# One gated hybrid decoder step on one core: shorter first steps of the triangular inverses, a guard folded into a multiplication, and two copies that change engines

## The chip, the core and the metric

The kernel runs on one core of a Trainium2 chip. The core has a matrix engine (TensorE, "PE" in the profile, with its weight loads listed apart as "PEld"), a vector engine (VectorE, "DVE"), a scalar engine for activation functions (ScalarE, "ACT"), a general engine (GpSimd, "POOL"), and a queue that issues transfers (SyncE, "SP"). They share an on-chip memory of 128 partitions (SBUF); matmuls write to a second one, PSUM, whose banks of 128 x 512 numbers are handed around by this program as buffers. The metric is the time of one execution on the device in microseconds, as a median over runs.

## The reference, cut to what matters

One layer is computed for a prompt of 1024 tokens and for eight samples of one token each. Width is 1024. A projection `p = x @ w_in` feeds a gated linear attention (GLA, 4 heads), an RWKV-7 recurrence (16 heads of 64) and two sigmoid gates; the two branches go through their own up-projections, are gated and added, pass an output product, and a layer norm ends it. The change lies in the RWKV branch:

```
w  = exp(-0.606531 * sigmoid(w0 + tanh(w_lr) @ w2));   a = sigmoid(a0 + a_lr @ a2)
kk = kb * k_k                                     # per head of 64 channels
kk = kk / maximum(sqrt(sum(kk**2)), 1e-12)
kb = kb * (1 + (a - 1) * k_a)
S_t = S_{t-1} (diag(w_t) - kk_t^T (kk_t * a_t)) + v_t^T k_t ;   y_t = S_t r_t
```

followed by a group norm of y, a bonus term and a gate.

## The kernel before, in words

**Tiling.** The tokens go in two passes: the first 512 prompt tokens with the eight samples (520 columns), then the other 512. Channels lie on the 128 partitions, tokens along the free dimension. A matmul with more precision than one multiplication of rounded numbers gives is made from two parts: the operand is rounded (the high part) and the rounding error is kept (the low part); the projections use three products, `hi*hi`, `hi*lo`, `lo*hi`. `split` (line 468) makes such a pair of parts: a copy that rounds, and a subtraction.

**The RWKV branch** works on pairs of heads: 8 pairs in each pass, 16 in all, each with 128 channels. `pair` (line 1111) runs four parts in turn.

- `front` (line 1135) makes the decay, the key norm and the operands of the chunked recurrence, in chunks of 64 tokens. `te` is the squared scaled key; `head_sums` (line 483) splits it and sums over each head by two matmuls with a matrix of ones, into a PSUM bank of the kind `big`, of which there are four. Line 1169 takes the larger of the sum and 1e-24, out of PSUM into `te`; then a logarithm and an exponential on ScalarE give the inverse square root (lines 1173 and 1174), scaled by 65536 under the logarithm. Line 1177 multiplies keys, `nkk` (the negated key scale `k_k`) and the inverse norm into `ta`; lines 1179 and 1180 make from it the first half of `AZ` and `td`.
- Still in `front`, Gram products of the chunks give triangular matrices, and their 32 x 32 diagonal blocks are gathered into a layout in which each partition holds one block. There, lines 1224 to 1229 invert all blocks at once in 31 steps: step j multiplies rows 0 to j of the inverse so far, cut into groups of which `ni = j // 4 + 1` are touched, by a row of the matrix (into `Xt`), and adds the product.
- `back` and `turn` join the blocks to 64 x 64 inverses and transpose operands.
- `chain` (line 1300) runs the recurrence over 8 chunks, each after the other: a matmul with the decayed products, its copy `rh` out of PSUM (line 1318), a matmul with the inverse, a copy to `u`, a matmul for the state, and the state update on VectorE. Copies of the state (`ss`, `s0p`) are ScalarE's.
- `norm` ends the pair and sends it to `o_rwkv` in device memory.

**Order.** Nothing is ordered by the hardware's choice alone. Each part above is a stream that yields instructions; `Order.run` (line 377) takes at each turn the stream whose next instruction can start first by its own estimated costs (`price`, line 145), corrected by a priority of the stream, and appends that instruction to its engine's list. So a changed instruction may change the order of all that is drawn after it, on every engine. `self.V`, `self.A` and `self.P` are VectorE, ScalarE and TensorE. `self.E` lets the planner choose VectorE or GpSimd for an instruction, and `self.C` ScalarE or VectorE, by which would end first by its estimate, where VectorE must be ahead of ScalarE by 0.1 us (`BIAS`). Activation functions belong to table sets; a change of set costs a table load on ScalarE (line 401), and sigmoid and exponential lie in different sets. Projection blocks are drawn between the steps of the chains and of the GLA heads, in PSUM banks of their own (`proj`).

Nearly all instructions are recorded at line 217, the helper that makes them, so groups of the profile are told apart by the names of their tiles.

Of the kernel before, what the change touches and what calls it, by code (L numbers as in the profile page):

```python
# [14 lines left out]
AF = mybir.ActivationFunctionType  # L15
ALU = mybir.AluOpType
# [16 lines left out]
C = 64  # L33
# [63 lines left out]
KK_SCALE = 65536.0  # L97
# [325 lines left out]
class Kern(Order):  # L423
# [41 lines left out]
        o, w = CST[name]  # L465
        return self.cons[:, o:o + w]

    def split(self, x, tag="part"):

        hi, lo = (t[:x.shape[0], :x.free_size()] for t in (yield from self.get(tag, 2)))  # L470
        yield self.C.copy(hi, x)
        yield (self.V if x.space == PSUM else self.E).tensor_sub(lo, x, hi.bitcast(F32))
        return hi, lo

# [5 lines left out]
    def blocks32(self, x):  # L480
        return x.rearrange("p (j f) -> p j f", f=32)

    def head_sums(self, x):

        hi, lo = yield from self.split(x)
        ps = yield from self.bank("big", [P, HT])
        yield from self.sums(ps, self.headsr, hi, lo)
        self.free(hi, lo)
        return ps
# [6 lines left out]
    def setup(self):  # L496
        nc, a = self.nc, self.a
        E = mybir.EngineType
        self.es.enter_context(self.tc.manual_schedule(engines={E.PE, E.Activation, E.DVE, E.Pool, E.SP}))
        cp = self.pool("const")  # L500
        wp = self.pool("w", side="left")
        self.dr = self.pool("dr", space=DRAM)
        pp = self.pool("psum", space=PSUM)
        xp = self.pool("x", side="right")
        self.r1 = r1 = self.pool("work", side="left")
        for tag, bufs in BANKS.items():
            self.buffers(tag, bufs, lambda tag=tag, bufs=bufs: pp.tile([P, 512], F32, name=tag, bufs=bufs))
        for tag, (shape, bufs) in SBUF.items():
            dt = F32R if tag in PARTS else F32
            self.buffers(tag, bufs, lambda tag=tag, shape=shape, bufs=bufs, dt=dt:  # L510
                         r1.tile(shape, dt, name=tag, bufs=bufs))
        for tag, (shape, bufs) in WBUF.items():
            dt = F32 if tag == "wraw" else F32R
            self.buffers(tag, bufs, lambda tag=tag, shape=shape, bufs=bufs, dt=dt:
                         wp.tile(shape, dt, name=tag, bufs=bufs))
        self.buffers("xs", XS, lambda: xp.tile([P, HALF], F32R, name="xs", bufs=XS))
        nc.scalar.preload_act_table_set(EXP)
        self.cons = cp.tile([P, CST_W], F32, name="cons")
        self.pv = cp.tile([P, PV_W], F32, name="pv")
        self.ident = self.cst("ident")  # L520
        self.omu = cp.tile([P, NRC], F32, name="omu")
        self.oka = cp.tile([P, 8], F32, name="oka")
        self.nkk = cp.tile([P, 8], F32, name="nkk")
        self.bias = {}
        for n, v in [("glaeps", GLA_EPS), ("gneps", GN_EPS), ("lneps", LN_EPS), ("one", 1.0),
                     ("kkl", 0.5 * math.log(KK_SCALE))]:
            t = cp.tile([P, 1], F32, name="b_" + n)
            nc.vector.memset(t, v)
            self.bias[n] = t
        dbg = getattr(self, "dbg", {})  # L530
        self.o_gla = dbg.get("o_gla", None) or self.dr.tile([D, T], F32, name="o_gla")
        self.o_rwkv = dbg.get("o_rwkv", None) or self.dr.tile([D, T], F32, name="o_rwkv")
        self.sg = [[[self.dr.tile([P, PASS[i][1]], F32, name=f"sg{i}{n}{k}") for k in range(NK)] for n in range(2)]
                   for i in range(2)]
        self.mg = [[self.dr.tile([P, PASS[i][1]], F32, name=f"mg{i}{k}") for k in range(NK)] for i in range(2)]

        self.lev = cp.tile([P, 2 * B32 * MASKED], U8, name="lev")

        self.onesr = cp.tile([P, P], F32R, name="onesr")
        self.headsr = cp.tile([P, P], F32R, name="headsr")  # L540
        self.wa = cp.tile([P, NK * 16], F32, name="wa")
        self.alr = cp.tile([96, HALF], F32R, name="alr")
        self.gw2 = cp.tile([96, GH * GDK], F32R, name="gw2")

        self.GS = [self.dr.tile([P, GDV], F32, name=f"GS{h}") for h in range(GH)]
        self.Sp = [self.dr.tile([P, C], F32, name=f"Sp{n}") for n in range(NPAIR)]

        self.smp = cp.tile([P, 4, NPAIR, NS], F32, name="smp")
        self.RS = self.dr.tile([4, NS, D], F32, name="RS")
        self.WA = self.dr.tile([2, NS, D], F32, name="WA")  # L550
        self.tail = cp.tile([P, NS + 1, NRC], F32, name="tail")
        self.carry = cp.tile([P, NRC], F32, name="carry")
        self.shT = cp.tile([P, NRC, NS], F32, name="shT")
        self.reset = cp.tile([P, HT], U8, name="reset")
        nc.vector.memset(self.reset, 1)
        nc.vector.memset(self.reset[:, ::C], 0)


        for tag, n, bufs in (("XT", 2 * HT, 2), ("X1", HT, 1), ("X2", HT, 1)):
            ts = [cp.tile([P, n], F32, name=f"{tag}{i}") for i in range(bufs)]  # L560
            for t in ts:
                nc.gpsimd.memset(t, 0.0)
            self.fixed(tag, ts)
# [571 lines left out]
    def front(self, c, p, st, d):  # L1135
        a, A, V, E = self.a, self.A, self.V, self.E
# [3 lines left out]
        AZ = az.rearrange("p (c k t) -> p c k t", c=NCH, k=2)  # L1140
# [11 lines left out]
        r, kb, v = (x[:, :HT] for x in st)  # L1152
        def bc(ap):
            return ap.rearrange("p (c t) -> p c t", t=C)
# [10 lines left out]
        yield from lora(pa, 1)  # L1165
        yield A.activation(td, pa, AF.Sigmoid, bias=self.pvec("a0", p))
        self.free(pa, l2h, l2l)
        ps = yield from self.head_sums(te)
        yield V.tensor_scalar(te, ps, 1e-24, None, ALU.max)
        self.free(ps)  # L1170
        yield V.tensor_tensor_scan(tb, self.reset, ta, 0.0, ALU.mult, ALU.add)
        yield E.memset(Pc[:, :, 0:1], 1.0)
        yield A.activation(te, te, AF.Ln, scale=KK_SCALE)
        yield A.activation(te, te, AF.Exp, scale=-0.5, bias=self.bias["kkl"])
        yield A.activation(Pc[:, :, 1:], bc(tb), AF.Exp, scale=-LAM)
        yield A.activation(tb, tb, AF.Exp, scale=LAM)
        yield V.scalar_tensor_tensor(ta, kb, self.nkk[:, p:p + 1], te, ALU.mult, ALU.mult)
        yield A.activation(te, td, AF.Identity, scale=self.pvec("ka", p), bias=self.oka[:, p:p + 1])
        yield E.tensor_mul(AZ[:, :, 0], bc(ta), Pc[:, :, 0:C])
        yield V.scalar_tensor_tensor(td, td, -1.0, ta, ALU.mult, ALU.mult)  # L1180
        yield E.tensor_mul(kb, kb, te)
        yield E.tensor_mul(AZ[:, :, 1], bc(r), Pc[:, :, 1:])
        pc = yield from self.get("pc")
# [39 lines left out]
        tm = yield from self.get("Xt")  # L1223
        for j in range(31):
            w, ni = 31 - j, j // 4 + 1
            tv = tm[:, :ni * w].rearrange("p (s t) -> p s t", t=w)
            yield V.tensor_mul(tv, X[:, 0:ni, j:j + 1].to_broadcast([P, ni, w]),
                               L[:, j:j + 1, j + 1:].to_broadcast([P, ni, w]))
            yield V.tensor_add(X[:, 0:ni, j + 1:], X[:, 0:ni, j + 1:], tv)
# [70 lines left out]
    def chain(self, c, p, d):  # L1300
# [12 lines left out]
        for x in range(NCH):  # L1313
            u = u_[:, x]
            pr = yield from self.bank("pch", [P, 2, C])
            yield self.P.matmul(pr, GG[:, x, 0], u, start=True, stop=True)
            rh = yield from self.get("rh")
            yield V.tensor_copy(rh, pr)
            self.free(pr)
            s0p = None  # L1320
            if x >= first:
                for h, hs in enumerate(HS):
                    yield A.copy(ss[hs, x], u[hs, h])
                s0p = yield from self.get("s0p")
                yield A.activation(s0p, ss[:, x], AF.Copy, scale=pc[:, x:x + 1])
            pu = yield from self.bank("pch", [P, 2, C])
            yield self.P.matmul(pu, XT[:, x], rh, start=True, stop=True)
            self.free(rh)
            for h, hs in enumerate(HS):
                yield self.C.copy(u[hs, h], pu[hs, h])  # L1330
            self.free(pu)
            pS = yield from self.bank("pch", [P, 2, C])
            yield self.P.matmul(pS, bt_[:, x], u, start=True, stop=True)
            for h, hs in enumerate(HS):
                un = u_[hs, x + 1, h] if x + 1 < NCH else S[hs]
                if s0p is None:
                    yield V.tensor_scalar(un, pS[hs, h], pc[hs, x:x + 1], None, ALU.mult)
                else:
                    yield V.scalar_tensor_tensor(un, pS[hs, h], pc[hs, x:x + 1], s0p[hs], ALU.mult, ALU.add)
            self.free(pS, *([] if s0p is None else [s0p]))  # L1340
# [499 lines left out]
```

## Time and profile before

| | |
|---|---|
| median of 3 runs | 1490.67 us (1490.38 to 1747.76) |
| the profiled execution | 1487.92 us |
| its span, first to last instruction | 1486.1 us |
| mean granted TensorE clock | 0.996 |
| instructions | 31563 |
| transfers | 318.96 MB in 211258 packets, mean 215 GB/s |

The span is the time between the first and the last instruction of the profiled execution; the execution's own time has some microseconds around it. In the views below, a row of a group gives: line, engine, operation, the tile written and the tiles read (buffer numbers left out), shapes, the count, the busy time in microseconds with the mean of one in nanoseconds, and the idle time of the engine just before, with what ended most of it. A row of the windows gives the busy time of each engine within a stretch of the span. A busy PE is not PE at its peak: matmuls are pipelined and their ends are modelled. Idle time of an engine that is not the bottleneck costs nothing.

The chain of waits that ended last names PE for most of its length from 1034 us on; the longest pieces of it after 1290 us are runs of 24 to 72 matmuls of the output products.

### The profile page before, as it was taken

The page shows a single profiled execution, that of the slowest core. Times are in us where ns is not written, and L with a number is a line of the kernel's source. Part 1 is how long each engine was busy: PE and PEld are TensorE (multiplying, and loading weights), DVE is VectorE, ACT ScalarE, POOL GpSimd, SP SyncE. Part 2 cuts the span into 40 slices and gives each one's busy share as a digit, 9 for nine tenths or more (in the row PEclk, how much of TensorE's full clock was granted, in tenths as well). Part 3 has the DMA queues.
Part 4 walks back from the last instruction along what each step waited for, and adds up shares of the span by engine and source line. Part 5 has one row for each costly group of instructions (what it writes and reads, how often), then busy time and mean ns, then how long its engine had stood idle before and what let it go on. Part 6 is the DMA issues. An engine that isn't in the chain of part 4 may idle for free. (4 is left out here: it accounts for less than half of the span.)

```text
span 1486.1 us, 31563 instructions
## 1 busy us (share of the span) xinstructions
PE 1449.8 (98%) x11158; PEld 1260.4 (85%) x11158; DVE 1194.8 (80%) x3255; ACT 857.7 (58%) x2196; POOL 113.6 (8%) x208
## 2 busy tenths in 40 slices
PE   9999999999999999999999999999999999999997
PEld 6998999899989998787777777878787898988786
DVE  6697889888998899879878989898877866755665
ACT  5666776676767776665754555474547645544210
POOL 1001010201010102000101020111001000000000
PEclk9999999999999999999999999999999999999999
DMA  8886786678676877566566556656564766888432
GB/s 299 273 285 202 250 296 214 226 253 295 202 258 211 294 229 258 170 224 188 160 198 179 155 190 191 192 154 188 174 189 138 229 210 221 295 293 271 139 107 85
DMA packets 211258, 318.96 MB, mean 215 GB/s; under 512 B 91811, under 2 KB 107180, under 8 KB 211100
## 3 DMA queue, kind: packets, MB, share of 16 engines
q1 hardware_dynamic: 211100, 316.93, 66.8%
q8 instruction: 89, 1.46, 0.4%
q14 instruction: 69, 0.57, 0.1%
HBM read 197.19 MB, written 118.61 MB: 212 GB/s over the span
## 5 line engine op out<-in xcount | busy, mean ns | idle before, releaser
L217 PE MATMUL proj<-xs,wpart 128*128 128x264 f32 (+2 forms) x5640 | 1017.7, 327 | 1.4 <-DVE row L217 0.8
L217 PEld LDWEIGHTS proj<-xs,wpart 128*128 128x128 f32 x5640 | 808.5, 189 | 80.3 <-issue 9.9
L217 ACT CAST wpart<-wraw 128x512 fp32r<-128x512 f32 x210 | 130.2, 623 | 103.5 <-PE proj L217 49.6
L217 DVE TENSOR_TENSOR row<-row 128x512 f32<-128x512 f32 (+7 forms) x321 | 166.3, 524 | 12.4 <-ACT row L217 5.6
L217 DVE TENSOR_TENSOR wpart<-wraw,wpart 128x512 fp32r<-128x512 f32 x207 | 145.2, 702 | 32.3 <-ACT wpart L217 31.4
L217 ACT ACTIVATE row<-row 128x512 f32<-128x512 f32 (+5 forms) x213 | 128.8, 610 | 14.4 <-DMA row<-sg 6.5
L217 POOL TENSOR_TENSOR row<-row 128x512 f32<-128x512 f32 (+5 forms) x64 | 72.7, 1143 | 746.3 <-DVE row L217 396.4
L217 DVE TENSOR_TENSOR Xt<-X,wide 128x60 f32<-128x60 f32 (+24 forms) x496 | 104.8, 211 | 11.7 <-DMA wide<-LD 1.8
L217 DVE TENSOR_TENSOR X<-X,Xt 128x60 f32<-128x60 f32 (+24 forms) x496 | 105.4, 213 | 10.0
L217 ACT ACTIVATE row<-proj,omu 128x256 f32<-128x256 f32 (+1 forms) x99 | 54.0, 546 | 93.5 <-PE proj L217 93.3
L217 PE MATMUL big<-xs,wpart 128*128 128x256 f32 (+2 forms) x576 | 101.7, 332 | 0.0
L217 PEld LDWEIGHTS big<-xs,wpart 128*128 128x128 f32 x576 | 87.7, 194 | 9.7 <-issue 0.2
L217 DVE SCALAR_TENSOR_TENSOR wide<-pch,pc,s0p 64x64 f32<-64x64 f32 x208 | 58.7, 282 | 32.9 <-PE pch L217 28.0
L217 ACT COPY row<-wide 64x64 f32<-64x64 f32 x240 | 57.9, 241 | 40.2 <-DVE wide L217 34.7
L401 ACT ACT_TABLE_LOAD x62 | 79.5, 1283 | 1.1
L217 DVE SCALAR_TENSOR_TENSOR row<-proj,pv,row 128x255 f32<-128x255 f32 (+1 forms) x99 | 56.3, 569 | 22.4 <-ACT tail L217 13.7
L217 PE MATMUL big<-row 128*32 128x32 f32 (+4 forms) x936 | 65.3, 241 | 1.4 <-ACT row L217 1.4
L217 ACT COPY row<-big 128x128 f32<-128x128 f32 (+6 forms) x134 | 38.7, 318 | 42.2 <-PE big L217 36.7
L217 ACT COPY wide<-pch 64x64 f32<-64x64 f32 x159 | 32.8, 206 | 47.0 <-PE pch L217 45.1
L217 ACT ACTIVATE row<-proj 128x128 f32<-128x128 f32 (+4 forms) x136 | 36.9, 324 | 37.4 <-PE proj L217 37.0
L217 PE MATMUL pch<-wide,gg 128*128 128x128 f32 x256 | 51.6, 283 | 5.5 <-DVE wide L217 4.7
L217 PEld LDWEIGHTS pch<-wide,gg 128*128 128x128 f32 x256 | 42.3, 189 | 16.1 <-PE proj L217 4.7
(249 smaller groups left out, 1992.6 us busy)
## 6 DMA issues: line engine op xcount, KB each, us to landing
w<-wpart SPq DMA_DIRECT2D x146, 512.0 KB
wpart<-w SPq DMA_DIRECT2D x146, 512.0 KB
wraw<-w_in SPq DMA_DIRECT2D x146, 256.0 KB
wide<-LD SPq DMA_DIRECT2D x64, 128.0 KB
wraw<-w_up_gla SPq DMA_DIRECT2D x32, 256.0 KB
wraw<-w_up_rwkv SPq DMA_DIRECT2D x32, 256.0 KB
sg<-row SPq DMA_DIRECT2D x16, 260.0 KB
row<-sg SPq DMA_DIRECT2D x16, 260.0 KB
```

Of the source, the lines that this page charges most:

```text
L217: ways.append((eng, lambda call=call: call(out, *args, **kw), price(eng, name, out, args, ins)))
L401: self.nc.scalar.preload_act_table_set(self.table)
```

## The change

Four edits, all in the RWKV branch.

1. **Inverse.** In steps 0 to 3, where one group of rows is touched, the multiplication into `Xt` and the addition become one `scalar_tensor_tensor` on VectorE: row j of the matrix times the j-th entry of the inverse's first row in that partition (a per-partition multiplier), plus the running row.
2. **Guard.** The maximum with 1e-24 goes. The logarithm reads the sums straight from PSUM, with a bias of 65536 x 1e-34; the bank is freed behind it. The guard is now a minimum with 1e12 on the inverse norm, inside the multiplication that makes `ta`; `ta` no longer holds `-k_k`, and that factor moves into the multiplications for the first half of `AZ` (a `scalar_tensor_tensor` on VectorE instead of a multiplication on VectorE or GpSimd) and for `td`.
3. **High part.** In the first `head_sums` of a pair the high part is no longer a rounding copy of `te` but a second Square of the keys on ScalarE, written in the rounded type.
4. **rh.** Its copy may go to ScalarE or VectorE, as the planner finds, instead of VectorE always.

```diff
-    def split(self, x, tag="part"):
+    def split(self, x, tag="part", high=None):
         hi, lo = (t[:x.shape[0], :x.free_size()] for t in (yield from self.get(tag, 2)))
-        yield self.C.copy(hi, x)
+        yield high(hi) if high else self.C.copy(hi, x)
         yield (self.V if x.space == PSUM else self.E).tensor_sub(lo, x, hi.bitcast(F32))
...
-    def head_sums(self, x):
-        hi, lo = yield from self.split(x)
+    def head_sums(self, x, high=None):
+        hi, lo = yield from self.split(x, high=high)
...
-                     ("kkl", 0.5 * math.log(KK_SCALE))]:
+                     ("kkl", 0.5 * math.log(KK_SCALE)), ("kkt", KK_SCALE * 1e-34)]:
...
-        ps = yield from self.head_sums(te)
-        yield V.tensor_scalar(te, ps, 1e-24, None, ALU.max)
-        self.free(ps)
+        ps = yield from self.head_sums(te, lambda hi: A.activation(hi, kb, AF.Square, scale=self.pvec("kk", p)))
         yield V.tensor_tensor_scan(tb, self.reset, ta, 0.0, ALU.mult, ALU.add)
         yield E.memset(Pc[:, :, 0:1], 1.0)
-        yield A.activation(te, te, AF.Ln, scale=KK_SCALE)
+        yield A.activation(te, ps, AF.Ln, scale=KK_SCALE, bias=self.bias["kkt"])
+        self.free(ps)
         yield A.activation(te, te, AF.Exp, scale=-0.5, bias=self.bias["kkl"])
...
-        yield V.scalar_tensor_tensor(ta, kb, self.nkk[:, p:p + 1], te, ALU.mult, ALU.mult)
+        yield V.scalar_tensor_tensor(ta, te, 1e12, kb, ALU.min, ALU.mult)
         yield A.activation(te, td, AF.Identity, scale=self.pvec("ka", p), bias=self.oka[:, p:p + 1])
-        yield E.tensor_mul(AZ[:, :, 0], bc(ta), Pc[:, :, 0:C])
-        yield V.scalar_tensor_tensor(td, td, -1.0, ta, ALU.mult, ALU.mult)
+        yield V.scalar_tensor_tensor(AZ[:, :, 0], bc(ta), self.nkk[:, p:p + 1], Pc[:, :, 0:C], ALU.mult, ALU.mult)
+        yield V.scalar_tensor_tensor(td, td, self.pvec("kk", p), ta, ALU.mult, ALU.mult)
...
         for j in range(31):
             w, ni = 31 - j, j // 4 + 1
+            if ni == 1:
+                yield V.scalar_tensor_tensor(X[:, 0, j + 1:], L[:, j, j + 1:], X[:, 0, j:j + 1], X[:, 0, j + 1:], ALU.mult, ALU.add)
+                continue
...
-            yield V.tensor_copy(rh, pr)
+            yield self.C.copy(rh, pr)
```

## The prediction

> **What bounds the kernel now.** I read the page first: the busy shares of the engines over the whole span.
>
> ```profile
> span 1486.1 us, 31563 instructions
> PE 1449.8 (98%) x11158; PEld 1260.4 (85%) x11158; DVE 1194.8 (80%) x3255; ACT 857.7 (58%) x2196; POOL 113.6 (8%) x208
> ```
>
> The matmuls leave 36.3 us of the span without PE work (1486.1 - 1449.8). A share over the whole span hides the stages, so the second view is the windows view, cut where the stages change: the body with projections, chains and GLA heads; the hundred microseconds of the last chain; the output products; the tail.
>
> ```profile
> 100.00:1200.00 1100.00, 1078.19 (x8751) 938.67 (x8750) 944.10 (x2750) 693.70 (x1827) 105.65 (x187) 1.00 0.67 210
> 1200.00:1300.00 100.00, 96.04 (x805) 92.24 (x804) 67.77 (x151) 55.19 (x110) 0.00 (x0) 0.97 0.77 248
> 1300.00:1440.00 140.00, 140.00 (x606) 111.09 (x605) 84.55 (x130) 48.05 (x100) 0.37 (x1) 1.00 0.63 210
> 1440.00:1486.00 46.00, 38.45 (x189) 31.93 (x188) 24.37 (x41) 1.99 (x8) 2.77 (x3) 0.96 0.26 86
> ```
>
> Columns: length, then busy time of PE, PEld, DVE, ACT, POOL, the granted clock, the DMA share and GB/s. PE is idle for 21.8 us of the body, 4.0 us around the last chain, never in the output products, and 7.6 us in the last stretch, where the last rows are normalised and stored. The change touches neither of the last two stages, so at most 25.8 us of idle time can answer to it. DVE is busy for 944.1 of 1100 us of the body: 86%, with 14% free.
>
> The third view is the list of waits of PE alone: what it stood idle for, in total, how often, and the longest.
>
> ```profile
> PE pch L217 <- DVE wide L217: 6.0, 9, 1.7
> PE pch L217 <- DVE rh L217: 4.1, 4, 1.8
> PE big L217 <- DVE part L217: 3.0, 5, 0.9
> PE big L217 <- DVE row L217: 2.2, 3, 1.3
> PE big L217 <- DVE X L217: 1.7, 1, 1.7
> PE big L217 <- DVE S L217: 1.1, 3, 0.5
> PE proj L217 <- DVE row L217: 0.8, 1, 0.8
> ```
>
> These seven rows, 18.9 us, are the time in which PE waited for VectorE. So the kernel is bound by PE, VectorE is the engine that PE waits for when it waits, and it waits little.
>
> **A page against a row.** The Trainium skill, in "Trainium Kernel Development and Optimization", Best Practices, says that matmul busy time is a poor measure and that weight-load busy time should be used. By that measure the 85% above would leave 225.7 us (1486.1 - 1260.4) for a faster feed to win. In the output products, where PE has no idle time at all, weight loads are busy for 111.09 of 140 us, 79%; so in this kernel 79% is already a full PE, and I give that room only a part of a rival's chance below.
>
> **One loss that is not idle time.** The granted clock of 0.97 in the second window sent me to shorter windows:
>
> ```profile
> 1236.00:1243.00 7.00, 6.49 (x30) 6.24 (x31) 2.84 (x7) 3.28 (x9) 0.00 (x0) 0.52 0.64 192
> ```
>
> After the idle stretches at the head of the last chain the clock is 0.52 for 7 us, which costs about 7 x 0.48 = 3.4 us of matmul time.
>
> **The change part by part.** Rows first: the inverse's removed pairs and the nearest row to what replaces them.
>
> ```profile
> L217 DVE TENSOR_TENSOR Xt<-X,wide 128x31 f32<-128x31 f32 x16 | 3.0, 185 | 1.9 <-DMA wide<-LD 1.8
> L217 DVE TENSOR_TENSOR X<-X,Xt 128x31 f32<-128x31 f32 x16 | 4.7, 292 | 0.8
> L217 DVE TENSOR_TENSOR Xt<-X,wide 128x28 f32<-128x28 f32 x32 | 7.0, 219 | 0.7
> L217 DVE TENSOR_TENSOR X<-X,Xt 128x28 f32<-128x28 f32 x32 | 5.9, 184 | 0.7
> L217 DVE SCALAR_TENSOR_TENSOR wide<-pch,pc,s0p 64x64 f32<-64x64 f32 x208 | 58.7, 282 | 32.9 <-PE pch L217 28.0
> ```
>
> *Inverse.* Steps 0 to 3 have one row block each, so eight instructions of a pair become four. The four rows average 220 ns, so 8 x 0.220 x 16 pairs = 28.2 us go. The new form, with a per-partition multiplier, costs between 185 ns (a two-input instruction of 31 elements) and 282 ns (the same form on 64 elements). I take 240, midway: 64 x 0.240 = 15.4 us. VectorE gains 12.8 us (10.1 to 16.4). Each step still needs the one before, and the last X leaves sooner by about 0.8 us a pair (12.8 / 16).
>
> ```profile
> L217 DVE TENSOR_SCALAR row<-big 128x512 f32<-128x512 f32 x16 | 11.0, 686 | 4.9 <-PE big L217 4.6
> L217 DVE CAST part<-row 128x512 fp32r<-128x512 f32 x31 | 14.8, 477 | 0.4
> L217 ACT CAST part<-row 128x512 fp32r<-128x512 f32 x7 | 4.3, 620 | 3.3 <-DVE row L217 2.4 <-DMA row<-w_out 0.9
> L217 ACT ACTIVATE row<-row,pv 128x512 f32<-128x512 f32 x16 | 11.6, 725 | 0.0
> L217 ACT ACTIVATE row<-row 128x512 f32<-128x512 f32 x120 | 75.3, 631 | 6.2 <-DVE row L217 2.9 <-DMA row<-sg 2.0
> L217 ACT ACTIVATE row<-big,b_glaeps 128x512 f32<-128x512 f32 x4 | 2.8, 688 | 0.1
> ```
>
> *Guard.* The max out of PSUM goes: VectorE -11.0 us. The logarithm then reads PSUM with a bias; the row of the same kind (688 against 631 ns) makes that 16 x 0.057 = +0.9 us on ScalarE.
>
> *High part.* 31 of 38 such copies lie on VectorE, so of the 16 that go I count 13 there, 13 x 0.477 = -6.2 us, and 3 on ScalarE, 3 x 0.620 = -1.9. A second Square of 725 ns comes in each pair: ScalarE +11.6, net +9.7. It needs only the keys, so it no longer waits for the first Square; the subtraction behind it waits for both.
>
> ```profile
> L217 DVE TENSOR_TENSOR az<-row 128x512 f32<-128x512 f32 x30 | 23.8, 793 | 1.3 <-ACT row L217 0.2
> L217 DVE SCALAR_TENSOR_TENSOR row<-row 128x512 f32<-128x512 f32 x20 | 14.8, 741 | 2.8 <-ACT row L217 2.6
> L217 DVE SCALAR_TENSOR_TENSOR row<-row,nkk 128x512 f32<-128x512 f32 x16 | 12.0, 747 | 6.4 <-ACT row L217 6.4
> L217 DVE SCALAR_TENSOR_TENSOR row<-row,pv 128x512 f32<-128x512 f32 x24 | 20.0, 835 | 0.2
> ```
>
> *Multiplications.* The min takes the place of a multiplier (747 to 741 ns, -0.1 us). td gets a multiplier (741 to between 747 and 835) and AZ's first half (793) becomes that form too. At the middle, 791, td costs 16 x 0.050 = 0.8 us and AZ nothing. AZ may no longer go to GpSimd: 30 of 32 were on VectorE, so at most two more, 1.6 us. Sum +2.3 us on VectorE (+0.0 to +3.6 with the ends, rounded).
>
> ```profile
> L217 DVE COPY rh<-pch 128x128 f32<-128x128 f32 x128 | 37.0, 289 | 17.5 <-PE pch L217 14.7
> L217 DVE COPY wide<-pch 64x64 f32<-64x64 f32 x97 | 21.4, 221 | 13.7 <-PE pch L217 11.3 <-issue 0.3
> L217 ACT COPY wide<-pch 64x64 f32<-64x64 f32 x159 | 32.8, 206 | 47.0 <-PE pch L217 45.1 <-DVE wide L217 0.3
> L217 ACT COPY row<-big 128x128 f32<-128x128 f32 x64 | 14.5, 268 | 17.8 <-PE big L217 17.6
> ```
>
> *rh.* The planner may choose, and takes VectorE only where it would end 0.1 us sooner. The copy of u in the same chain has that choice already and went to ScalarE 159 times of 256, 62%. By that share 80 of the 128 copies move: VectorE -80 x 0.289 = -23.0 us (0 to -37.0), ScalarE +80 x 0.268 = +21.3. The copy itself is hardly shorter; what it gains is the engine that is free first. On ScalarE it now stands ahead of the copies of the state and of the weights' high parts, which wait for it, and they in turn feed later work only.
>
> VectorE's sum is -12.8 - 11.0 - 6.2 + 2.3 - 23.0 = -50.7 us, to 1144; ScalarE's is +0.9 + 9.7 + 21.3 = +31.9, to 890, or 60% of the span. PE keeps every instruction, and no transfer is added, dropped or moved.
>
> **From busy time to time.** One row of a view by tile places the sixteen fronts (two head sums of two matmuls in each of 16 pairs):
>
> ```profile
> L217 PE MATMUL big<-part,headsr x64: 388/398/584, 44.9 to 1150.6; 128*128 128x512 f32 x64
> ```
>
> One front lies ahead of the body and one chain behind it, so 15/16 of the 50.7 us, 47.5, fall in the body: VectorE's share there goes from 86% to 81.5% (896.6 / 1100). An instruction meets a busy engine less often: busy over free falls from 6.06 to 4.41, by 27%. I let PE's waits for VectorE shrink by as much, which is a choice: 0.27 x 18.9 = 5.1 us. The profiled execution took 1487.92 us, 1.8 more than its span, and the median, 1490.67, lies 2.8 above that; the gain carries over as microseconds. 1490.67 - 5.1 = 1486. All else that VectorE saves is hidden under PE's 98%. The order is planned by estimated times, so every engine's list is drawn anew; a third of the 25.8 us of idle time, 8 us either way, is my allowance for that draw: 1478 to 1494.
>
> **The rivals.**
>
> *Slower: the bank is held.* Today VectorE empties the PSUM bank of the head sums at once. The timeline of one pair:
>
> ```profile
> 990.44 0.69 DVE L217 TENSOR_SCALAR row<-big 128x512 f32<-128x512 f32 x1
> 992.11 1.28 ACT L401 ACT_TABLE_LOAD   x1
> 993.40 0.63 ACT L217 ACTIVATE row<-row 128x512 f32<-128x512 f32 x1
> ```
>
> The bank comes free at 991.13. With the logarithm reading it, it comes free at 994.03, after the table load: 2.9 us later. So the max was not the last thing waited for, and the pair's front is hardly shorter. There are four such banks, and the Gram products behind want two, the GLA chunks one or two. If they stood still each time, 16 x 2.9 = 46 us; most of that PE fills with projections in their own banks, as the 98% shows. At a quarter unfilled it is 12 us, less the gain of 5.1: +7, 1498. It decides once more than a ninth of that time (5.1 of 46) is unfilled.
>
> *Much faster.* If VectorE's queue also holds back weights and operands where no idle time shows, half of all that could go (25.8 + 3.4 = 29.2) is 15 us: 1476. Against it: 18.9 us is all that PE waits for VectorE.
>
> *The clock.* With a smoother start of the last chain the slow-clock stretch does not occur: 3.4 us, and with part of that window's 4.0 us of idle some 5 in all: 1481. It needs a luckier draw, as rh is one of several things late there. The Trainium skill, "TensorE: Matmul & The Clock Gate", Part 1, has the clock as either full or half, half after an idle window of some 3.4 us; the trace agrees with half, and shows it after broken idling and not after one long gap.
>
> *It does not do what it says.* rh stays on VectorE: its sum is -27.7 us, 26 of them in the body, the share 83.5%, busy over free 5.05, the waits shrink by 17%: 3.2 us, 1487.
>
> **How the numbers follow.** Forecast 0.45 at 1486 (its own 1478 to 1494); rh stays 0.10 at 1487; clock 0.12 at 1481; much faster 0.13 at 1476; bank held 0.20 at 1498. From 1474 to 1500 holds the time 8 times in 10: what is left out is the far half of the much faster case and the third of the slow one in which more of the held time is unfilled. 2% is 29.8 us, about what a measurement of this kernel can tell from no change. Faster by that would need all of the 29.2 us and more: 0.02. Slower by that would need most of the 46 us: 0.02. Within: 0.96.
>
> **What would show it.** Right: PE within 1 us of 1449.8 busy; VectorE at 1130 to 1160 and ScalarE at 875 to 905; rh on both engines; the waits of PE for VectorE near 14 us. The new inverse step shows its price as a form of its own. The bank rival shows as PE rows `big` waiting for ScalarE, and as a longer idle time in the body with VectorE less busy. I am wrong if VectorE drops by 50 us and PE's idle time does not move, or if the time moves by more than the idle time does.

## The result

The changed kernel takes 1478.69 us (median of 6 runs) against 1490.53 us for the kernel before (6 runs). The ratio is 0.9925, with a 95% interval of 0.9904 to 0.9946: some 12 us, 0.75%, faster. The forecast was 1486, its range 1474 to 1500. One of the six executions of the kernel before took 1747.76 us, far longer than the other five, and the ratio leaves it out. So the direction and the range held, and the gain was more than twice the 5 us of the sum. The experiments below show that the reason given for those 5 us does not hold.

The profiled execution of the changed kernel, first its page:

```profile
span 1476.5 us, 31483 instructions
PE 1446.6 (98%) x11158; PEld 1258.8 (85%) x11158; DVE 1163.0 (79%) x3071; ACT 878.9 (60%) x2302; POOL 108.8 (7%) x205
```

The span is 9.6 us shorter. 6.4 us of that is idle time of PE (36.3 to 29.9 us), 3.2 us is time in which PE counts as busy. The prediction had named, as a sign that it is wrong, that the time moves by more than the idle time does: 9.6 us against 6.4 is that sign. The same stages as before, in the windows view (length; busy PE, PEld, DVE, ACT, POOL; granted clock; DMA share; GB/s):

```profile
100.00:1200.00 1100.00, 1082.56 (x8793) 944.36 (x8793) 916.88 (x2578) 714.80 (x1923) 100.84 (x184) 1.00 0.67 212
1200.00:1300.00 100.00, 97.99 (x791) 92.19 (x790) 66.20 (x139) 57.32 (x123) 0.00 (x0) 0.98 0.82 261
1300.00:1440.00 140.00, 140.00 (x606) 111.12 (x606) 86.24 (x133) 44.61 (x95) 0.37 (x1) 1.00 0.59 198
1440.00:1476.50 36.50, 28.76 (x148) 24.14 (x146) 19.15 (x32) 1.49 (x6) 2.77 (x3) 0.96 0.25 81
```

PE's idle time in the body went from 21.8 to 17.4 us, around the last chain from 4.0 to 2.0, and in the tail it is what it was (7.6 and 7.7). A gain in the body appears here as a head start: 8793 matmuls are done in the window from 100 to 1200 us instead of 8751. PE's largest waits for VectorE in the changed kernel, and one for a transfer (1.2 us before):

```profile
PE pch L217 <- DVE wide L217: 3.3, 8, 0.9
PE big L217 <- DVE part L217: 1.7, 4, 0.7
PE big L217 <- DVE S L217: 1.6, 2, 1.3
PE big L217 <- DVE row L217: 1.3, 3, 0.8
PE big L217 <- DVE l2p L217: 1.3, 2, 0.9
PE big L217 <- DVE X L217: 1.3, 1, 1.3
PE big L217 <- DMA X<-XD: 2.1, 1, 2.1
```

No row for `rh` is left. All rows of waits for VectorE, the smallest too, add up to 12.9 us; in the kernel before they are 20.6, since the seven rows of the prediction, 18.9 us, leave out four small ones of 1.7 us together. The instructions of the change, by shape:

```profile
L217 DVE SCALAR_TENSOR_TENSOR X<-wide,X 128x31 f32<-128x31 f32 (+1 forms) x64 | 16.6, 259 | 4.9 <-DMA wpart<-w 2.4 <-DMA wide<-LD 0.5
L217 DVE COPY rh<-pch 128x128 f32<-128x128 f32 x24 | 7.0, 290 | 4.5 <-PE pch L217 4.0
L217 ACT COPY rh<-pch 128x128 f32<-128x128 f32 x104 | 27.5, 264 | 84.8 <-PE pch L217 83.8
L217 ACT ACTIVATE part<-row,pv 128x512 fp32r<-128x512 f32 x16 | 11.6, 723 | 0.0
L217 ACT ACTIVATE row<-big,b_kkt 128x512 f32<-128x512 f32 x16 | 11.0, 688 | 0.7 <-PE big L217 0.6
L217 DVE SCALAR_TENSOR_TENSOR az<-row,nkk 128x512 f32<-128x512 f32 x16 | 13.5, 843 | 1.3 <-ACT row L217 0.6
```

The new inverse step costs 259 ns, `rh` is on ScalarE 104 times of 128, and the second Square and the logarithm out of PSUM cost what the nearest rows of before said (723 and 688 ns).

### The profile page after: what moved, and what is told of

Same layout as the page of the kernel before. It is cut to its first block, busy times and chain, and to the rows that moved or that the text cites. A ratio compares the mean times of both kernels' runs of the same rounds, so it can differ in the third digit from the quotient of the medians.

```text
span 1476.5 us, 31483 instructions
## 1 busy us (share of the span) xinstructions
PE 1446.6 (98%) x11158; PEld 1258.8 (85%) x11158; DVE 1163.0 (79%) x3071; ACT 878.9 (60%) x2302; POOL 108.8 (7%) x205
## 4 chain that ended last, share of the span: by engine, by line
PE 77%; DVE 14%; ACT 3%; DMA 2%; issue 2%; SPq 1%; POOL 0%; POOLq 0%; DVEq 0%; ACTq 0%
PE proj L217 48%; PE big L217 20%; DVE row L217 6%; PE pch L217 5%; PE pY L217 4%; ACT row L217 2%; DVE X L217 1%; DVE wide L217 1%; DVE Xt L217 1%; SPq L217 1%; DVE pair L217 1%; ACT L401 1%; DVE az L217 1%; DVE bk L217 1%; DVE ac L217 1%
## 5 line engine op out<-in xcount | busy, mean ns | idle before, releaser
L217 DVE TENSOR_TENSOR row<-row 128x512 f32<-128x512 f32 (+8 forms) x327 | 173.1, 537 | 13.0 <-ACT row L217 6.6
L217 ACT CAST wpart<-wraw 128x512 fp32r<-128x512 f32 x210 | 129.6, 622 | 89.7 <-PE proj L217 36.3
L217 DVE TENSOR_TENSOR wpart<-wraw,wpart 128x512 fp32r<-128x512 f32 x198 | 137.2, 695 | 34.4 <-ACT wpart L217 32.0
L217 ACT ACTIVATE row<-row 128x512 f32<-128x512 f32 (+3 forms) x197 | 117.6, 606 | 13.0 <-DVE row L217 4.1
L217 PE MATMUL big<-xs,wpart 128*128 128x512 f32 (+2 forms) x576 | 102.9, 332 | 0.8 <-DVE xs L217 0.7
L217 DVE TENSOR_TENSOR Xt<-X,wide 128x60 f32<-128x60 f32 (+21 forms) x432 | 94.7, 219 | 9.4
L217 POOL TENSOR_TENSOR row<-row 128x512 f32<-128x512 f32 (+7 forms) x58 | 60.2, 1043 | 536.7 <-DVE row L217 190.5
L217 DVE TENSOR_TENSOR X<-X,Xt 128x60 f32<-128x60 f32 (+21 forms) x432 | 91.8, 212 | 9.7
L217 PEld LDWEIGHTS big<-xs,wpart 128*128 128x128 f32 x576 | 87.0, 191 | 11.9 <-DVE xs L217 1.6
L217 ACT COPY rh<-pch 128x128 f32<-128x128 f32 x104 | 27.5, 264 | 84.8 <-PE pch L217 83.8
L217 ACT COPY row<-big 128x128 f32<-128x128 f32 (+7 forms) x144 | 41.1, 308 | 51.5 <-PE big L217 43.2
L217 ACT CAST xs<-row 128x520 fp32r<-128x520 f32 (+1 forms) x64 | 38.4, 622 | 29.2 <-PE proj L217 10.3
```

Source lines behind the costliest of these rows:

```text
L217: ways.append((eng, lambda call=call: call(out, *args, **kw), price(eng, name, out, args, ins)))
```

## The experiments

Three theories were held against each other. *VectorE*: the time comes from the work taken off VectorE, each edit in proportion. *Draw*: the time comes from the newly drawn order, which any edit sets off. *Chain*: it comes from `rh`, which no longer queues on VectorE. A table of all kernels; ratios are to the kernel before on the same chip, the other columns from each one's profiled execution, PE idle being the span less PE's busy time. The kernel before itself had medians from 1486.93 to 1490.53 us in the four series of runs, and a profile is one execution; so spans of different rows are compared only roughly, and the ratio decides. (For "before, redrawn 2" the profiled execution was the fastest of twelve.)

| kernel | ratio, 95% interval | span | PE idle | VectorE busy |
|---|---|---|---|---|
| before | 1 | 1486.1 | 36.3 | 1194.8 |
| changed | 0.9925 (0.9904 to 0.9946) | 1476.5 | 29.9 | 1163.0 |
| inverse alone | 0.9969 (0.9956 to 0.9982) | 1481.7 | 35.5 | 1191.3 |
| guard alone | 0.9929 (0.9915 to 0.9942) | 1477.3 | 31.3 | 1182.1 |
| high part alone | 0.9943 (0.9930 to 0.9956) | 1478.3 | 29.8 | 1190.0 |
| rh alone | 1.0021 (1.0011 to 1.0031) | 1489.7 | 37.8 | 1172.5 |
| before, redrawn 1 | 1.0077 (1.0056 to 1.0099) | 1494.0 | 41.3 | 1196.5 |
| before, redrawn 2 | 1.0026 (1.0009 to 1.0042) | 1485.0 | 37.6 | 1181.6 |
| changed, redrawn 1 | 0.9931 (0.9912 to 0.9950) | 1477.4 | 31.1 | 1161.7 |
| changed, redrawn 2 | 1.0107 (1.0085 to 1.0128) | 1500.5 | 49.4 | 1147.7 |
| order of changed, old work | 1.0077 (1.0060 to 1.0094) | 1497.0 | 38.5 | 1204.4 |
| order of before, new work | 1.0018 (1.0004 to 1.0031) | 1488.0 | 36.9 | 1158.0 |
| order of before, light VectorE | 0.9937 (0.9917 to 0.9957) | 1479.0 | 33.7 | 1062.8 |
| order of before, rh on ScalarE | 1.0004 (0.9992 to 1.0016) | 1486.2 | 37.0 | 1173.0 |

### Each edit alone

**Inverse alone.**

```diff
             w, ni = 31 - j, j // 4 + 1
+            if ni == 1:
+                yield V.scalar_tensor_tensor(X[:, 0, j + 1:], L[:, j, j + 1:], X[:, 0, j:j + 1], X[:, 0, j + 1:], ALU.mult, ALU.add)
+                continue
```

> The kernel before with the inverse edit alone: steps 0 to 3 as one instruction each. Theory VectorE (the gain of 11.8 us comes from taking work off VectorE, each edit in proportion to its VectorE time): of my sum of 50.7 us this edit has 12.8, so about 3 us faster, 1487 to 1488, VectorE busy 10 to 16 us less. Theory draw (what moved the time is mainly the newly drawn order, which any edit sets off): anywhere from 1480 to 1497, with no relation to the VectorE time saved. Theory chain (the gain is rh's, whose copy no longer queues on VectorE): no change beyond 2 us, 1488 to 1492.

**Guard alone.** The lines of the change's second edit, with the high part, the inverse and `rh` as before.

```diff
         ps = yield from self.head_sums(te)
-        yield V.tensor_scalar(te, ps, 1e-24, None, ALU.max)
-        self.free(ps)
...
-        yield A.activation(te, te, AF.Ln, scale=KK_SCALE)
+        yield A.activation(te, ps, AF.Ln, scale=KK_SCALE, bias=self.bias["kkt"])
+        self.free(ps)
...
+        yield V.scalar_tensor_tensor(ta, te, 1e12, kb, ALU.min, ALU.mult)
```

> The kernel before with the guard edit alone: no maximum, the logarithm reads PSUM with a bias and holds the bank, the minimum inside the multiplication. Theory VectorE: 11.0 us off and 2.3 on, so about 2 us faster, 1488 to 1489. Rival bank held: the bank stays taken some 3 us longer in each of 16 pairs, 3 to 12 us slower, 1494 to 1503, with more idle time of PE in front of matmuls into big. Theory draw: anywhere from 1480 to 1497. Theory chain: 1488 to 1492.

**High part alone.**

```diff
-        yield self.C.copy(hi, x)
+        yield high(hi) if high else self.C.copy(hi, x)
...
-        ps = yield from self.head_sums(te)
+        ps = yield from self.head_sums(te, lambda hi: A.activation(hi, kb, AF.Square, scale=self.pvec("kk", p)))
         yield V.tensor_scalar(te, ps, 1e-24, None, ALU.max)
```

> The kernel before with the high-part edit alone: a second Square of the keys on ScalarE in place of the rounding copy. Theory VectorE: 6.2 us off VectorE, about 1.5 us faster, 1489. Theory draw: anywhere from 1480 to 1497. Theory chain: 1488 to 1492. ScalarE busy about 10 us more in all of them.

**rh alone.**

```diff
-            yield V.tensor_copy(rh, pr)
+            yield self.C.copy(rh, pr)
```

> The kernel before with the rh edit alone: its copy on ScalarE or VectorE. Theory VectorE: 100 of 128 copies move (as in the changed kernel, which shows 104), 29 us off VectorE, more than half of all, so 5 to 7 us faster, 1484 to 1486. Theory chain: the whole gain, 10 to 12 us faster, 1479 to 1481, and PE no longer waits for rh. Theory draw: anywhere from 1480 to 1497.

The second line of each one's page, in the order of the four:

```profile
PE 1446.2 (98%) x11158; PEld 1259.2 (85%) x11158; DVE 1191.3 (80%) x3168; ACT 869.4 (59%) x2233; POOL 101.7 (7%) x198
```
```profile
PE 1446.0 (98%) x11158; PEld 1260.6 (85%) x11158; DVE 1182.1 (80%) x3223; ACT 869.1 (59%) x2228; POOL 99.1 (7%) x197
```
```profile
PE 1448.5 (98%) x11158; PEld 1261.7 (85%) x11158; DVE 1190.0 (81%) x3249; ACT 856.9 (58%) x2207; POOL 98.1 (7%) x197
```
```profile
PE 1451.9 (97%) x11158; PEld 1263.4 (85%) x11158; DVE 1172.5 (79%) x3146; ACT 872.3 (59%) x2301; POOL 115.7 (8%) x212
```

`rh` takes 22.3 us off VectorE's busy time, more than the other three together (3.5, 12.7 and 4.8), and is the only one that comes out slower. The inverse's 3.5 us were to be 10 to 16; other work moved onto VectorE. The high part, which takes 4.8 us off and did not even add to ScalarE (856.9 against 857.7, where 10 more were expected), gains 0.6%. In its order ScalarE has 57 table loads instead of 63, which alone is 7.7 us less. Proportion to VectorE's time is gone. For the chain theory one draw is not enough, but `rh` shows no gain in this draw and none in the order of before, at the end of this section. Added up, the four are 0.9862 (1 - 0.0031 - 0.0071 - 0.0057 + 0.0021), nearly twice the change's own gain, so they are not pieces of one sum either.

The rival of the held bank can be read in the guard edit, which alone holds the bank. Its time (the fastest of the four) does not settle it, since its order is new too. Its waits do: a matmul that waited for a bank held by the logarithm would wait for ScalarE's `row`, and that row is as large as in before (1.4 us both; 1.0 in the changed kernel). The bank's longer stay did not cost the 3 to 12 us that it was priced at.

```profile
PE big L217 <- ACT row L217: 1.4, 2, 0.8
```

### Nothing but the order

If the order is the cause, it must move the time with no edit of the work at all. These four change one number of the planner's estimates by 2 to 3%, and thereby the order. With it the planner also picks another engine for some of the copies that may go to two: before, redrawn 2, has 36 instructions fewer on VectorE than before and 33 more on ScalarE. So "order" here is the whole plan, the place and the engine.

```diff
-        return 0.068 + wide / (480 if name == "copy_predicated" else 960) + 0.06 * scalars
+        return 0.070 + wide / (480 if name == "copy_predicated" else 960) + 0.06 * scalars
...
-        return 0.097 + n / 1200 + (0.042 if len(src) == len(ins) else 0.0) + 0.094 * extra
+        return 0.099 + n / 1200 + (0.042 if len(src) == len(ins) else 0.0) + 0.094 * extra
```

The first line makes "redrawn 1", the second "redrawn 2", each in the kernel before and in the changed kernel.

> The kernel before, with nothing changed but the planner's estimate of a VectorE instruction, 0.070 in place of 0.068 us fixed cost: the same instructions on the data, in a newly drawn order. Theory draw: the time moves by some microseconds with no edit at all, 3 to 10 us either way, 1481 to 1500. Theory VectorE: within 3 us of before, 1488 to 1494, since VectorE's busy time stays within a few microseconds of 1195.

> The kernel before, with only the planner's estimate of a ScalarE instruction changed, 0.099 in place of 0.097 us. Theory draw: 3 to 10 us either way, and not where the first redraw came out. Theory VectorE: 1488 to 1494.

> The changed kernel, with only the planner's estimate of a VectorE instruction changed, 0.070 in place of 0.068 us. Theory VectorE: it keeps the gain, 1476 to 1482. Theory draw: the gain of 11.8 us was in good part one lucky order, and this comes out 3 to 10 us away from 1479, more likely above: 1482 to 1489.

> The changed kernel, with only the planner's estimate of a ScalarE instruction changed, 0.099 in place of 0.097 us. Theory VectorE: 1476 to 1482. Theory draw: 3 to 10 us away from 1479, more likely above: 1482 to 1489.

Three orders of the old work give 1, 1.0026 and 1.0077; three of the new work 0.9925, 0.9931 and 1.0107. The first redraw of the changed kernel came out where the VectorE theory had it (1477.04 us), the second far above what either theory had (1502.33); the first redraw of before is inside the draw theory's range alone (1499.07), the second (1489.91) inside both. The spread from the order alone is 27 us with the new work (0.0182 x 1490.5), more than twice the change's gain, and 11 us with the old. The slowest of all has the least VectorE time of the six. It has 19.5 us more idle time of PE than the changed kernel, 11.9 of them between 1200 and 1300 us. Where it loses most, in the list of PE's waits between 1180 and 1260 us, and in the windows view around it:

```profile
PE big L217 <- DMA X<-XD: 10.8, 1, 10.8
PE big L217 <- DVE row L217: 2.0, 1, 2.0
```
```profile
1215.00:1218.58 3.58, 1.07 (x8) 0.62 (x6) 2.80 (x6) 1.91 (x6) 0.00 (x0) 1.00 0.52 108
1218.58:1235.65 17.07, 6.40 (x51) 5.48 (x52) 4.98 (x11) 5.31 (x12) 0.00 (x0) 0.50 0.68 191
1235.65:1239.00 3.35, 3.35 (x29) 3.35 (x29) 0.42 (x1) 1.31 (x4) 0.00 (x0) 1.00 0.02 5
```

In this order PE runs out of other matmuls behind the last pair's inverse, and stands for 10.8 us until the inverse's blocks have been stored and gathered again; the clock is at half for 17 us around it, in which PE is busy for 6.4. Redrawn 2 of before has such a place too, with another cause:

```profile
PE pch L217 <- ACT row L217: 7.2, 1, 7.2
```

### The work changed, the order held

The last four kernels keep the planner's list and change only what is issued at a place of it. The planner still sees the instruction of the one kernel; the other's is issued instead:

```diff
+def instead(op, fn=None, first=None):
+    op.ways = [(e, (lambda f=f: ((first() if first else None), (fn or f)())), c) for e, f, c in op.ways]
+    return op
...
-            yield V.tensor_copy(rh, pr)
+            yield instead(V.tensor_copy(rh, pr), lambda: self.nc.scalar.copy(rh, pr))
```

The second part is the kernel with `rh` on ScalarE. "New work" has that, and these two:

```diff
-        yield self.C.copy(hi, x)
+        yield instead(self.C.copy(hi, x), high and (lambda: high(hi)))
...
+            if ni == 1:
+                instead(mul, lambda: None)
+                instead(add, lambda j=j: self.nc.vector.scalar_tensor_tensor(X[:, 0, j + 1:], L[:, j, j + 1:], X[:, 0, j:j + 1], X[:, 0, j + 1:], ALU.mult, ALU.add))
             yield mul
             yield add
```

"Light VectorE" issues nothing for the steps behind the fourth, so it leaves the inverses unfinished:

```diff
+            if j > 3:
+                instead(mul, lambda: None)
+                instead(add, lambda j=j: None)
             yield mul
             yield add
```

"Old work" goes the other way, from the changed kernel; a part of it:

```diff
-        yield E.memset(Pc[:, :, 0:1], 1.0)
-        yield A.activation(te, ps, AF.Ln, scale=KK_SCALE, bias=self.bias["kkt"])
+        yield instead(E.memset(Pc[:, :, 0:1], 1.0), first=lambda: self.nc.vector.tensor_scalar(te, ps, 1e-24, None, ALU.max))
+        yield instead(A.activation(te, ps, AF.Ln, scale=KK_SCALE, bias=self.bias["kkt"]), lambda: self.nc.scalar.activation(te, te, AF.Ln, scale=KK_SCALE))
...
-            yield self.C.copy(rh, pr)
+            yield instead(self.C.copy(rh, pr), lambda: self.nc.vector.tensor_copy(rh, pr))
```

> The order of the changed kernel, kept instruction for instruction on PE, SyncE and GpSimd, but at each changed place the old instructions: two per inverse step, the maximum (issued beside the small memset behind it), the rounding copy and rh on VectorE, the old multiplications. So VectorE gets back some 45 to 60 us of work and the order is the lucky one. Theory VectorE: the gain goes, 1487 to 1491. Theory draw: the time stays near the changed kernel's, 1478 to 1482. My prediction's rule (PE's waits follow busy over free of VectorE): about 5 us more than the changed kernel, 1483 to 1485.

> The order of the kernel before, kept on PE, SyncE and GpSimd, with three of the four edits' instructions in it: one instruction per inverse step 0 to 3, the second Square on ScalarE for the high part, rh always on ScalarE. The maximum stays. VectorE loses about 55 us (12.8 + 6.2 + 37.0 by the prediction's terms). Theory VectorE: the full gain, 10 to 12 us faster than before, 1476 to 1479. Theory draw: within 3 us of before, 1484 to 1491. The prediction's rule: about 5 us faster, 1482 to 1484.

> The order of the kernel before, kept, with steps 4 to 30 of the inverses left out (54 of 62 VectorE instructions in each of 16 pairs, some 180 us of VectorE time, 15%), so the inverses are not completed and the output is not the reference's. It bounds what any relief of VectorE can win while the order stays. Theory VectorE: 20 to 26 us faster, since nearly all of PE's waits go, 1461 to 1468. Theory draw: well under half of that, 1478 to 1484, because the list of PE places the work where the planner thought the inverse would end.

> The order of the kernel before, kept, with rh always on ScalarE: 37 us off VectorE and 34 us more on ScalarE, at the planned places. rh alone with a new order came out 0.2% slower than before. Theory VectorE: 6 to 9 us faster, 1479 to 1482. Theory draw (the 0.2% was the order, and rh itself is worth little): within 2 us of before, 1485 to 1489. Rival ScalarE (rh now queues behind 0.6 us copies and table loads of 1.28 us, and the chain is late): 3 us slower or more, with PE's waits in front of the matmul that reads rh put down to ScalarE.

*Order of before, light VectorE.* 132 us less of VectorE's busy time, four times what the change takes off, and PE's largest waits for VectorE are those of before:

```profile
PE 1445.2 (98%) x11158; PEld 1260.9 (85%) x11158; DVE 1062.8 (72%) x2391; ACT 855.2 (58%) x2196; POOL 112.8 (8%) x208
PE pch L217 <- DVE wide L217: 6.7, 10, 1.4
PE pch L217 <- DVE rh L217: 3.1, 5, 1.3
PE big L217 <- DVE part L217: 3.1, 5, 1.1
```

The same three rows were 6.0, 4.1 and 3.0; all rows for VectorE are 18.6 us, and were 20.6. The kernel is 0.6% faster, 9 us, where the VectorE theory had 20 to 26. The draw theory's 1478 to 1484 holds it. But 9 us is near what the prediction's rule, applied to this kernel, would give: VectorE's share of the body is 74.5% (819.49 / 1100), busy over free falls by 52%, and 0.52 x 18.9 is 9.8 us. So the time alone does not speak against the rule; the waits do, which fell by 2 us. Of the 7.1 us by which the span is shorter 4.6 lie in PE's busy time, and what made them is not known.

The body of the three kernels in the order of before, in the windows view (light VectorE, new work, `rh` on ScalarE):

```profile
100.00:1200.00 1100.00, 1080.25 (x8794) 944.59 (x8793) 819.49 (x1925) 694.16 (x1828) 104.86 (x187) 1.00 0.68 211
100.00:1200.00 1100.00, 1078.12 (x8699) 937.49 (x8698) 904.08 (x2528) 718.49 (x1954) 105.23 (x187) 1.00 0.67 209
100.00:1200.00 1100.00, 1077.14 (x8719) 937.15 (x8718) 920.85 (x2615) 710.89 (x1939) 104.79 (x187) 1.00 0.67 210
```

*Order of before, new work.* 37 us less VectorE, and no gain (1.0018). `rh` no longer shows among PE's waits, but the second Square, issued on ScalarE at places that were planned for a copy mostly on VectorE, now does (line 1174 is that Square in this kernel):

```profile
PE 1451.1 (98%) x11158; PEld 1261.7 (85%) x11158; DVE 1158.0 (78%) x3048; ACT 887.2 (60%) x2339; POOL 113.2 (8%) x208
PE big L217 <- ACT part L1174: 4.8, 8, 1.2
PE pch L217 <- DVE wide L217: 4.8, 7, 1.1
```

All waits for VectorE fell here, from 20.6 to 16.0 us, about as the rule has it (busy over free down by 24%, 4.5 us); all waits for ScalarE rose by more, from 3.5 to 9.0. So this kernel shows that the three edits win nothing when put into the old order, and not that VectorE's relief does nothing. The guard edit, the fastest alone, is not in it: what that one is worth in a held order was not tried.

*Order of before, rh on ScalarE.* The same time as before (1.0004), as the draw theory had it, with 22 us less VectorE and 21 us more ScalarE. One wait for `rh` is left, put down to ScalarE, of 1.0 us. By the rule the waits for VectorE would have fallen by 15%, 2.9 us; they are 21.0 us, against 20.6, because those for `wide`, the tile that takes the state update and the copy of `u`, grew from 6.0 to 9.2 us as those for `rh` went.

*Order of the changed kernel, old work.* This went against both theories' numbers, far above: 1.0077, or 22.7 us more than the changed kernel (1.0077 less 0.9925, times 1490.5), for 41 us more VectorE time.

```profile
PE 1458.5 (97%) x11158; PEld 1259.2 (84%) x11158; DVE 1204.4 (80%) x3271; ACT 847.2 (57%) x2182; POOL 108.5 (7%) x205
PE pch L217 <- DVE wide L217: 8.3, 20, 0.8
100.00:1200.00 1100.00, 1075.39 (x8620) 925.66 (x8619) 937.97 (x2704) 677.53 (x1796) 100.55 (x184) 1.00 0.66 208
```

PE's wait for `wide` goes from 8 times to 20 and from 3.3 to 8.3 us, and 173 fewer matmuls are done in that window than in the changed kernel (8620 against 8793); 11.9 us of the loss is in PE's busy time, 8.6 us in its idle time. So the two directions are not alike: taking work out of the order that was planned with it won nothing, or 9 us for 132 us less; putting work into an order planned without it costs 23 us. They are not mirror images either: the old work has all four edits undone, with the maximum behind the scan instead of ahead of it and all sixteen high parts on VectorE. That a list written for later results simply waits at the places it was written for, while one written for earlier results is late everywhere, fits both; it was not shown, and which instructions make the 23 us was not tried.

## Why the prediction was right or wrong

**What bounds the kernel: right.** PE stays at 98%, with every matmul kept; the output products have no idle time; nearly all of the idle time that went lay in the body and around the last chain. PE's busy time moved by 3.2 us where I allowed 1. About 1.5 us of it is the clock: the stretch at half clock went from 6.83 us, 6.32 of them busy, to 3.42, with 3.24 busy. The rest of the 3.2 us is not explained.

```profile
1236.27:1243.10 6.83, 6.32 (x30) 6.08 (x29) 2.64 (x8) 3.04 (x8) 0.00 (x0) 0.50 0.66 199
```
```profile
1231.46:1234.88 3.42, 3.24 (x15) 3.25 (x16) 2.59 (x8) 1.35 (x3) 0.00 (x0) 0.50 0.38 109
```

**The terms on VectorE: right in sum as durations, wrong as busy time.** The durations of all VectorE records add up to 1316.1 us before and 1266.4 after: 49.7 us less, and the sum was 50.7. That they agree so well is partly luck, as the parts show. But the busy time fell by 31.8, to 1163.0, past the 1160 that I had named. Instructions that do not wait for one another can overlap in the records, and the busy time counts the overlap once: 121.3 us of it before, 103.4 after. A removed copy that stood among others frees less than its own duration. In the timeline of before:

```profile
1006.70 0.69 DVE L217 TENSOR_TENSOR gg<-big,cons 128x512 f32<-128x512 f32 x1
1007.30 0.28 DVE L217 COPY rh<-pch 128x128 f32<-128x128 f32 x1
1007.50 0.68 DVE L217 TENSOR_TENSOR gg<-big,cons 128x512 f32<-128x512 f32 x1
```

The copy starts 0.09 us before the product ahead of it ends, and the next starts 0.08 us before the copy ends: of its 0.28 us some 0.2 pass between the two starts. I had multiplied counts by durations throughout. The parts: the inverse's new steps cost 16.6 us where I expected 15.4, and all rows of its tiles together fell by 7.2 us where I expected 12.8; `rh` took 30.0 us off with 104 copies where I expected 23.0 with 80. These two misses cancel. The first half of `AZ` cost 843 ns a piece, above the range I gave it (747 to 835). ScalarE's +31.9 became +28.7 in durations, since the planner moved other copies the other way and needed two table loads less, and +21.2 in busy time.

**From busy time to time: wrong.** "I let PE's waits for VectorE shrink by as much" is the step that fails. Within the order of before, VectorE at 1062.8 us busy leaves PE's waits for it near where they were (18.6 us, from 20.6, where the rule has half), and `rh` on ScalarE leaves them at 21.0. Most of that waiting was not for want of free VectorE time. The fall of the waits to 12.9 us in the changed kernel (10.5 in the six rows shown, the rest in smaller ones) is what I had named as what would show the step right. It follows the order and not VectorE's load: the waits are 12.1 us with the high part alone, with only 4.8 us less VectorE time, 14.4 with the old work in redrawn 2 of before, and 21.5 in redrawn 2 of the changed kernel, which has the least VectorE time of these. And the prediction put nothing down for PE's busy time, which made a third of the gain in the span.

**The allowance for the draw: too small.** I gave 8 us either way, a third of PE's idle time. Three orders of the new work spread over 27 us. The result lies inside even the forecast's own 1478 to 1494, just above its lower end; with orders this far apart that was partly luck. So the gain of 12 us is real for this kernel, but it hangs on the order. Two of the three orders of the new work have it, and the third loses more than it: with the new work the three orders average 0.9988, with the old 1.0034, and with so few of each the difference cannot be told from none. Whether shorter instructions give better orders on average stays open.

**The rivals.** *The bank is held*: did not come; PE's waits for ScalarE's `row` did not grow. *Much faster*, at 1476, came near the figure, but its reason can be worth little here: 132 us less VectorE time won 9 us in the light kernel, and the change takes 31.8 us off. *The clock*, at 1481, came half: of a stretch of two times 3.4 us one went, and another order brought 17 us of half clock. The Trainium skill, "TensorE: Matmul & The Clock Gate", Part 1, describes the clock as full or half, in windows of 3.4 us; the runs agree, with 0.50 and lengths of 3.42, 6.83 and 17.07 us, which are 1, 2 and 5 times 3.41. What the Trainium skill calls the condition, an idle window, is met most plainly in the 10.8 us wait above; in before, broken idling was enough (PE busy for 1.08 of the last 3.37 us at full clock). *It does not do what it says*: no, 104 of 128 copies moved. The Trainium skill's measure by weight-load time ("Trainium Kernel Development and Optimization", Best Practices) reads 85% in the kernel before and 85% in the changed one, and did not tell the two apart.

## What to carry to other kernels

Where a planner draws the whole order anew, redraw both kernels a few times with nothing changed but one estimate before you credit an edit with a difference; here that alone was worth 27 us with the new work and 11 with the old, and the edit 12. To learn what an edit is worth by itself, hold the order and change only what is issued; then see too what new waits the fixed places make, as the second Square did. A wait of the bottleneck engine for another engine does not mean that the other is short of time: take a large piece of its work away and see whether the wait goes.

## What the runs showed of the hardware

Records of consecutive VectorE instructions overlap: in the kernel before 1497 of them begin before the one ahead of them has ended, half of them by 82 ns or more. In the inverse, where one needs the other's result, they do not: of the 221 additions of the inverse that directly follow the multiplication whose product they read, none begins early. So the durations of one engine's records can add up to 10% more than its busy time (1316.1 against 1194.8 us). And a scalar_tensor_tensor with a per-partition multiplier on 28 to 31 elements costs 259 ns on the mean, against 282 ns for one on 64 elements that reads PSUM, and against some 213 ns, the mean of their rows, for each of the two plain instructions whose place it takes.
